# Moving GpSimd's element-wise work to VectorE in a two-layer hybrid decoder trunk

## The chip, the cores and the metric

The kernel runs on one core of a Trainium2 chip. The metric is the device time of one execution in microseconds; the median of several runs counts. The engines are called as the profile calls them: PE is TensorE (PEld its weight loads), DVE is VectorE, ACT is ScalarE, POOL is GpSimd, SP is SyncE, which issues the DMAs.

## The reference, cut to what matters

Two layers over 256 tokens of width 1024, all in float32. Each layer has four parts, each behind an RMSNorm and added to the residual stream:

```python
for i in range(DEPTH):
    h = h + 0.5 * swiglu(rms_norm(h, ffn1_norm[i]), ffn1_w_gate_up[i], ffn1_w_down[i])
    h = h + parallel_mixing(rms_norm(h, mix_norm[i]), mix_w_in[i], ...)
    h = h + memory_cross_attention(rms_norm(h, xa_norm[i]), rms_norm(mem, xa_mem_norm[i]), ...)
    h = h + 0.5 * swiglu(rms_norm(h, ffn2_norm[i]), ffn2_w_gate_up[i], ffn2_w_down[i])
return rms_norm(h, final_norm)
```

The mixing part is the one that matters here. It projects to three head groups, whose results are joined and projected back:

- A, a gated delta net with 4 heads of 128 in chunks of 64: a short causal convolution and silu on q, k and v, l2 normalization of q and k, beta = sigmoid, g = -exp(a_log) * softplus(a + dt_bias), per chunk the inverse of a unit lower triangular 64x64 matrix (`triangular_solve`), a state carried from chunk to chunk, then an RMSNorm with `dn_out_norm` (one gain for each of the 128 columns of a head) and a product with silu(z);
- B, softmax attention in three dilated windows, 4 heads of 64;
- C, spatial gating: gelu, a layer norm with gain and bias, a lower triangular 128x128 matrix for each of 4 groups, a product.

## The kernel before, in words

Activations lie transposed, features on the 128 partitions and the 256 tokens along the free dimension. All large products take weights that come from HBM in chunks of 128x2048 in two tiles `wr`. Each tile is split into a high part `wh` (ACT casts it to the faster matmul type fp32r) and a low part `wl` (raw minus high, one DVE tensor_tensor of 1024 columns); three matmuls, high by high, high by low and low by high, then give float32 accuracy. `wsplit`, `wchunk` and `pair` (line 770) do this; `pair` takes one chunk and makes two 128x256 results with 48 matmuls. Small products of the delta net run as plain float32 matmuls on PE (kind "f", or "fs" with 64 columns), those of weights as kind "r".

The program isn't emitted in the order in which it is written. Every operation is recorded by `Plan.add` (line 162) with an estimated time on its engine (`dur`) and until its result can be read (`lat`, for DVE 0.08 us longer than `dur`). `Plan.schedule` (line 190) is a list planner: it simulates the five engines, at every step takes the engine that can start first and among its ready operations the one with the highest rank (the length of the chain behind it). Its result is the fixed instruction order of each engine; the chip then keeps each engine's order and waits on semaphores. The planner holds off an operation with two SBUF operands on DVE while one runs on POOL and the other way round (`lock`, kind "2"), charges PE for going from kind "r" to "f" and back (`switch`, line 266), and can lower the rank of an operation that would make PE change its kind by `HOLD` (line 147, used in line 303; 0.0 here). Every instruction is emitted at line 369, so rows of the trace are told apart by tiles, not by lines.

POOL has these jobs on data, all in the mixing part (`mixing`, line 843): the low part of the second tile of six chunks in each layer (`pair(x, (None, GP))`, lines 854 and 920), the low parts of the memory keys (line 827), the products of the decay matrix E with the key norms (line 983), the masks `mb` for the five later rounds of the triangular inverse (line 1024), the scaling of the softmax (line 1151), the masked spatial weights (line 1187), gain and bias of the layer norm (lines 1201 and 1202) and the out gain on z (line 1227). It also sets small tiles to constants and computes x to the power -1/2 for the norms (`rsqrt`, line 632), on at most 8 columns.

The triangular inverse runs in rounds over blocks of 2 to 32 (LEVELS). A round has for each of two token tiles: four small products of `mb` with `tt` on PE (the trace's ps<-tc,Mb), two ACT copies into the halves of `q` (Q<-ps), four small products (ps<-Q,uc), two DVE subtractions on the two halves of the partitions (tc<-tc,ps) and four DVE transposes on the four blocks of 32 partitions (uc<-tc). The other weight chunks of the mixing part are there to fill PE meanwhile. `proj_add` ends the part and takes the delta net's four results last.

Of the kernel before, what the change touches and what calls it, by code (L numbers as in the profile page):

```python
# [10 lines left out]
F32 = mybir.dt.float32  # L11
F32R = mybir.dt.float32r
# [34 lines left out]
S_DT, S_AL = 88, 92  # L47
S_BA = 96
NS = S_BA

L_ZG, L_LG, L_LB, L_BS, L_WS = 0, 128, 384, 640, 896
NL = L_WS + 512
# [83 lines left out]
class Plan:  # L136
# [9 lines left out]
    KEEP = ("pg", "ps", "wh", "wl", "t")  # L146
    HOLD = 0.0

# [13 lines left out]
    def add(self, eng, method, args, kw, outs, ins, dur, lat, table=None, kind=None):  # L162
        i = len(self.ops)
        op = dict(i=i, eng=eng, method=method, args=args, kw=kw, dur=dur, lat=lat, table=table, kind=kind,
                  prio=self.boost, tiles=[], preds={}, succs=[])
        for views, wr in ((ins, False), (outs, True)):
# [23 lines left out]
    def schedule(self, fixed=None):  # L190
# [37 lines left out]
        dma_next, table, kind, feed = 0, None, None, 0.0  # L228
        lock = {"DVE": 0.0, "GP": 0.0}
        dmas = [o["i"] for o in ops if o["eng"] == "DMA"]  # L230
        for o in ops:
# [43 lines left out]
        while left:  # L275
            best = None
            for e, lst in ready.items():
# [7 lines left out]
                for o in lst:  # L285
                    st = slot_time(o)
                    if st is not None:
                        t = max(o["at"], st, free[e])
                        if o["kind"] == "2":
                            t = max(t, lock["GP" if e == "DVE" else "DVE"])  # L290
                        cands.append((t, o))
                if not cands:
# [31 lines left out]
            if o["kind"] == "2":  # L324
                lock[e] = t + dur
            ready[e].remove(o)
            if fixed:
# [16 lines left out]
            for j in o["succs"]:  # L344
                q = ops[j]
                q["at"] = max(q["at"], end + self.hop(o, q))
                q["n"] -= 1
                if not q["n"]:
                    ready[q["eng"]].append(q)
# [135 lines left out]
def trunk(tc, xT, memT, w, w2, ca_d, cb_d, sm_d, fin_d, lb_d, out):  # L485
    plan = Plan(tc)
    PE, ACT, DVE, GP, SY = Tensor(plan), Scalar(plan), Vector(plan, "DVE"), Vector(plan, "GP"), Queue(plan)
    with ExitStack() as ctx:
# [331 lines left out]
        def mem_keys(xm):  # L820
            rb = mem_r[1][0]
            KT = []
            for c in range(4):
                ps = pair(xm)
                k = S([2, T])
                DVE.tensor_tensor(k, ps, bc4(rb, 2), op=ALU.mult)
                KT.append(parts(k, GP))
            return KT
# [14 lines left out]
        def mixing(l, norm, nxt, xm):  # L843
# [9 lines left out]
            pgv = xstat256(x, [wsplit(raw) for raw in raws], 264)  # L853
            pk0 = pair(x, (None, GP))
            r, (rb, rb8) = norm.st.finish("h", (1.0, 0.125))
# [61 lines left out]
            def conv(n, ps0=None):  # L917
                res = []
                for c in range(2):
                    ps = ps0 if ps0 is not None and c == 0 else pair(x, (None, GP))  # L920
                    for e in range(2):
# [59 lines left out]
            for t in range(2):  # L981
                es = E[t]
                GP.tensor_tensor(es, es, bcl(rk[:, 4 * t:4 * t + 4]), op=ALU.mult)
                pb = hmm(lambda o, i: PE.matmul(
# [35 lines left out]
            for n, b in enumerate(LEVELS[1:]):  # L1020
                for t in range(2):
                    u, tt, q = Uc[t], Tc[t], Qc[t]
                    mb = plan.tile([P, NH, 64], F32, "Mb", 6)
                    GP.tensor_tensor(mb, Mc[t], bc4(cbs(C_LVL + 64 * (n + 1), 64)), op=ALU.mult)
                    ps = sbank([NH, 64])
# [108 lines left out]
            for t in (1, 0):  # L1134
                nk = P * (t + 1)
                for par in range(2):
# [13 lines left out]
                    DVE.reciprocal(den, den)  # L1150
                    GP.tensor_tensor(p, p, bcl(den, nk), op=ALU.mult)
                    for i in range(2):
# [19 lines left out]
            def gelu2(z):  # L1172
# [13 lines left out]
            wsm = S([NH, P])  # L1186
            GP.tensor_tensor(wsm, lb[:, L_WS:L_WS + 512].rearrange("p (a b) -> p a b", a=4),
                             bc4(cbs(C_TRIU)), op=ALU.mult)
            ps = sbank([2, T])
            for t in range(2):  # L1190
# [8 lines left out]
                DVE.tensor_scalar(rs, rs, 0.5, None, op0=ALU.mult)  # L1199
                DVE.tensor_scalar(gv_[:, t, :], gv_[:, t, :], mv[:, 0:1], rs, op0=ALU.subtract, op1=ALU.mult)  # L1200
                GP.tensor_tensor(gv_[:, t, :], gv_[:, t, :], lb[:, L_LG:L_LG + T], op=ALU.mult)
                GP.tensor_tensor(gv_[:, t, :], gv_[:, t, :], lb[:, L_LB:L_LB + T], op=ALU.add)
                for gi in range(NH):
# [16 lines left out]
            for t in range(2):  # L1220
                z = S([NH, P])
                zf = z.rearrange("p a b -> p (a b)")
                act(zf, pp[t], AF.Copy, scale=r[:, t:t + 1])
                th = S([NH, P])
                act(th, z, AF.Tanh, scale=0.5)
                DVE.scalar_tensor_tensor(z, th, 1.0, z, op0=ALU.add, op1=ALU.mult)
                GP.tensor_tensor(z, z, bc4(lb[:, L_ZG:L_ZG + P]), op=ALU.mult)
                zg.append(z)
# [4 lines left out]
            for c in range(2):  # L1233
                ps = sbank([2, T])
                for e in range(2):
                    for t in range(2):
                        PE.transpose(ps[:, e, tsl(t)], zg[t][:, 2 * c + e, :], ident)
                sh, sl = parts(ps)
                merged[2 * c:2 * c + 2] = [(sh[:, i, :], sl[:, i, :]) for i in range(2)]
# [78 lines left out]
def _pack(a):  # L1318
# [23 lines left out]
    for l in range(DEPTH):  # L1342
# [23 lines left out]
        for half in range(2):  # L1366
# [8 lines left out]
        al = np.broadcast_to(f["dn_a_log"][l], (P, 4))  # L1375
        small.append(np.concatenate(gc + [cw, dt, al], 1))
        bs = f["sg_b_spatial"][l]
        big.append(np.concatenate([
            np.broadcast_to(f["dn_out_norm"][l], (P, P)),
            np.broadcast_to(f["sg_norm_gain"][l], (P, T)),  # L1380
# [49 lines left out]
```

## Time and profile before

| | us |
|---|---|
| median of 3 runs | 1286.95 (1285.84 to 1287.96) |
| profiled execution | 1287.47 |
| its span | 1285.70 |
| PE busy | 1253.5 |
| DVE busy | 957.5 |
| ACT busy | 718.4 |
| POOL busy | 120.8 |

The granted TensorE clock is at its upper level through nearly all of the span. The span begins with the FFN of layer 0; the mixing part of layer 0 lies from about 200 to 375 us, that of layer 1 from about 830 to 1005 us, and POOL's work on data lies in these two. A row of a group gives engine, operation, output and inputs by tile names with their shapes, the count, the busy time and the mean time of one; a row of the timeline gives the start and the time taken by the instructions merged in it. A matmul is listed longer than it keeps PE, since the next one starts before it ends.

### The profile page before, as it was taken

How to read it: one execution, taken by the hardware profiler on the slowest of the kernel's cores; microseconds unless marked ns; L12 is line 12 of the kernel's file. 1: busy time of each engine (PE TensorE's matmuls, PEld its weight loads, DVE VectorE, ACT ScalarE, POOL GpSimd, SP SyncE). 2: the span in 40 equal slices, each digit the busy share in tenths (PEclk: the TensorE clock that was granted, in tenths of full speed). 3: DMA queues.
4: the chain of work that ended last, by engine and by line, in shares of the span. 5: the costliest groups of instructions: out<-in, count | busy, mean ns of one | idle time of the engine just before them, and what ended most of it. 6: DMA issues, size and time to landing. Idle time of an engine off the chain costs nothing.

```text
span 1285.7 us, 22163 instructions
## 1 busy us (share of the span) xinstructions
PE 1253.5 (97%) x8376; PEld 1129.8 (88%) x8376; DVE 957.5 (74%) x1711; ACT 718.4 (56%) x1286; POOL 120.8 (9%) x135
## 2 busy tenths in 40 slices
PE   7999999999999999999999999998999999999997
PEld 6888889988998988888988888998899989888886
DVE  6777867987775777777677776699867766777764
ACT  6565745735654565555456565466366455555552
POOL 1000002441300000000000000036022000000000
PEclk9999999999999999999999999999999999999998
DMA  6555764423345455556555566643243544555551
GB/s 223 192 189 199 243 204 162 151 99 115 116 165 164 130 177 186 192 172 202 189 180 189 189 200 201 212 163 103 98 132 118 182 161 130 182 182 195 182 193 68
DMA packets 60874, 216.27 MB, mean 168 GB/s; under 512 B 7136, under 2 KB 7520, under 8 KB 60640
## 3 DMA queue, kind: packets, MB, share of 16 engines
q1 hardware_dynamic: 60768, 214.86, 50.5%
q8 instruction: 66, 1.08, 0.4%
q14 instruction: 40, 0.33, 0.1%
HBM read 213.78 MB, written 1.05 MB: 167 GB/s over the span
## 4 chain that ended last, share of the span: by engine, by line
PE 57%; issue 16%; DVE 7%; ACT 1%; DMA 0%; POOL 0%; POOLq 0%; DVEq 0%; SPq 0%; ACTq 0%
PE pg L369 51%; PE ps L369 6%; DVE wl L369 2%; DVE S L369 1%; DVE uc L369 1%; DVE q L369 1%; DVE tc L369 1%; ACT wh L369 1%; DMA S<-memT 0%; POOL wl L369 0%; DVE xs L369 0%; DVE po L369 0%; DVE zz L369 0%; DVE xmx L369 0%; ACT S L369 0%
## 5 line engine op out<-in xcount | busy, mean ns | idle before, releaser
L369 DVE TENSOR_TENSOR wl<-wr,wh 128x1024 fp32r<-128x1024 f32 (+1 forms) x386 | 479.0, 1242 | 231.1 <-ACT wh L369 230.2
L369 ACT CAST wh<-wr 128x1024 fp32r<-128x1024 f32 (+2 forms) x398 | 415.0, 1044 | 418.2 <-issue 254.4
L369 PE MATMUL pg<-X,wh 128*128 128x512 f32 (+1 forms) x2240 | 635.9, 354 | 6.7 <-DVE t L369 6.5
L369 PE MATMUL pg<-X,wl 128*128 128x256 f32 x1824 | 485.1, 282 | 6.0 <-POOL xs L369 2.6
L369 PEld LDWEIGHTS pg<-X,wh 128*128 128x128 f32 x2240 | 382.2, 189 | 53.6 <-ACT wh L369 6.5
L369 PE MATMUL pg<-S,wh 128*128 128x256 f32 (+1 forms) x1560 | 386.7, 327 | 0.0
L369 PEld LDWEIGHTS pg<-X,wl 128*128 128x128 f32 x1824 | 344.5, 189 | 24.4 <-DVE wl L369 4.1
L369 PE MATMUL pg<-S,wl 128*128 128x256 f32 x1088 | 301.9, 282 | 0.5 <-DVE wl L369 0.5
L369 PEld LDWEIGHTS pg<-S,wh 128*128 128x128 f32 x1560 | 260.2, 189 | 24.9
L369 PEld LDWEIGHTS pg<-S,wl 128*128 128x128 f32 x1088 | 205.0, 188 | 3.9 <-DVE wl L369 1.5
L369 DVE TENSOR_TENSOR t<-t,pg 128x256 f32<-128x256 f32 x204 | 84.1, 415 | 3.4 <-ACT t L369 3.4
L369 ACT COPY t<-pg 128x256 f32<-128x256 f32 x204 | 73.9, 366 | 15.1 <-PE pg L369 15.1
L369 DVE TENSOR_TENSOR t<-t,t 128x256 f32<-128x256 f32 x157 | 66.0, 422 | 10.9 <-ACT t L369 3.0
L369 POOL TENSOR_TENSOR rch<-rv,one 128x2 f32<-128x2 f32 x9 | 7.4, 821 | 631.5 <-DVE rv L369 631.5
L369 DVE TENSOR_TENSOR t<-t,rbh 128x256 f32<-128x256 f32 x116 | 48.4, 420 | 0.9
L369 PE MATMUL pg<-wh,X 128*128 128x264 f32 (+2 forms) x192 | 47.4, 332 | 0.0
L369 PE MATMUL ps<-S,S 128*128 128x256 f32 (+4 forms) x384 | 47.0, 289 | 0.0
L369 PEld LDWEIGHTS ps<-S,S 128*128 128x128 f32 (+2 forms) x384 | 41.4, 178 | 2.6 <-issue 1.0
L369 ACT CAST S<-t 128x256 fp32r<-128x256 f32 x88 | 35.8, 408 | 10.1 <-DVE t L369 10.1
L369 ACT ACTIVATE t<-t 128x256 f32<-128x256 f32 x88 | 36.5, 420 | 7.8 <-DVE t L369 7.7
L369 PE MATMUL pg<-wh,S 128*128 128x512 f32 x128 | 40.6, 393 | 0.0
L369 DVE TENSOR_TENSOR S<-t,S 128x256 fp32r<-128x256 f32 x88 | 36.8, 419 | 1.9 <-ACT S L369 1.9
(175 smaller groups left out, 966.6 us busy)
## 6 DMA issues: line engine op xcount, KB each, us to landing
wr<-w SPq DMA_DIRECT2D x390, 512.0 KB, 3.3
wr<-w SPq DMA_DIRECT2D x4, 528.0 KB, 4.6
S<-memT SPq DMA_DIRECT2D x8, 256.0 KB, 6.4
lb<-lb SPq DMA_DIRECT2D x2, 704.0 KB, 6.5
one<-cb SPq DMA_DIRECT2D x1, 1248.0 KB, 6.1
one<-xT SPq DMA_DIRECT2D x4, 256.0 KB, 5.3
wr<-w SPq DMA_DIRECT2D x4, 256.0 KB, 5.5
out<-S SPq DMA_DIRECT2D x3, 256.0 KB, 2.4
```

The source lines that it names most:

```text
L369: getattr(self.engines[o["eng"]], o["method"])(*[real(a) for a in o["args"]], **{k: real(a) for k, a in o["kw"].items()})
```

## The change

All listed jobs of POOL go to DVE, except the out gain on z: that comes in as a per-partition scalar (`S_ON`) when the transposed z is copied out of PSUM, ACT taking the high part with a scale and DVE the low part with a scalar_tensor_tensor. The layer norm's gain and bias are worked into two scalar_tensor_tensor, in place of one tensor_scalar on DVE and two operations on POOL. POOL keeps the memsets and the powers. In the planner, DVE and ACT no longer start an operation on other partition rows than the one before until that one has ended (`rows`, `over`); HOLD goes from 0 to 2 us; and a PE result counts as ready for the next PE instruction as soon as PE is free.

```diff
-    HOLD = 0.0
+    HOLD = 2.0
@@ add
-                  prio=self.boost, tiles=[], preds={}, succs=[])
+                  prio=self.boost, tiles=[], preds={}, succs=[], rows=outs[0].box()[0:2] if isinstance(outs[0], View) else None)
@@ schedule
         lock = {"DVE": 0.0, "GP": 0.0}
+        rows, over = {"DVE": None, "ACT": None}, {"DVE": 0.0, "ACT": 0.0}
...
+                        if e in rows and rows[e] != o["rows"]:
+                            t = max(t, over[e])
...
+            if e in rows:
+                rows[e], over[e] = o["rows"], t + lat + 0.02
...
-                q["at"] = max(q["at"], end + self.hop(o, q))
+                q["at"] = max(q["at"], t + dur if e == q["eng"] == "PE" else end + self.hop(o, q))
@@ mem_keys
-                KT.append(parts(k, GP))
+                KT.append(parts(k))
@@ mixing
-            pk0 = pair(x, (None, GP))
+            pk0 = pair(x)
...
-                    ps = ps0 if ps0 is not None and c == 0 else pair(x, (None, GP))
+                    ps = ps0 if ps0 is not None and c == 0 else pair(x)
...
-                GP.tensor_tensor(es, es, bcl(rk[:, 4 * t:4 * t + 4]), op=ALU.mult)
+                DVE.tensor_tensor(es, es, bcl(rk[:, 4 * t:4 * t + 4]), op=ALU.mult)
...
-                    GP.tensor_tensor(mb, Mc[t], bc4(cbs(C_LVL + 64 * (n + 1), 64)), op=ALU.mult)
+                    DVE.tensor_tensor(mb, Mc[t], bc4(cbs(C_LVL + 64 * (n + 1), 64)), op=ALU.mult)
...
-                    GP.tensor_tensor(p, p, bcl(den, nk), op=ALU.mult)
+                    for i in range(2):
+                        DVE.tensor_scalar(p[:, i, :], p[:, i, :], den[:, i:i + 1], None, op0=ALU.mult)
...
-            GP.tensor_tensor(wsm, lb[:, L_WS:L_WS + 512].rearrange("p (a b) -> p a b", a=4),
+            DVE.tensor_tensor(wsm, lb[:, L_WS:L_WS + 512].rearrange("p (a b) -> p a b", a=4),
                              bc4(cbs(C_TRIU)), op=ALU.mult)
...
-                DVE.tensor_scalar(gv_[:, t, :], gv_[:, t, :], mv[:, 0:1], rs, op0=ALU.subtract, op1=ALU.mult)
-                GP.tensor_tensor(gv_[:, t, :], gv_[:, t, :], lb[:, L_LG:L_LG + T], op=ALU.mult)
-                GP.tensor_tensor(gv_[:, t, :], gv_[:, t, :], lb[:, L_LB:L_LB + T], op=ALU.add)
+                DVE.scalar_tensor_tensor(gv_[:, t, :], gv_[:, t, :], mv[:, 0:1], lb[:, L_LG:L_LG + T],
+                                         op0=ALU.subtract, op1=ALU.mult)
+                DVE.scalar_tensor_tensor(gv_[:, t, :], gv_[:, t, :], rs, lb[:, L_LB:L_LB + T],
+                                         op0=ALU.mult, op1=ALU.add)
...
-                GP.tensor_tensor(z, z, bc4(lb[:, L_ZG:L_ZG + P]), op=ALU.mult)
...
-                sh, sl = parts(ps)
+
+                g = smc[:, S_ON:S_ON + 1]
+                sh, sl = S([2, T], F32R), S([2, T], F32R)
+                act(sh, ps, AF.Copy, scale=g)
+                DVE.scalar_tensor_tensor(sl, ps, g, sh.bitcast(F32), op0=ALU.mult, op1=ALU.subtract)
```

The packing on the host moves `dn_out_norm` from the table `lb` (128 columns less) to the table `sm` (one column more).

## Rows read from the trace of the kernel before

**Rows 1.** The page: busy time of each engine, share of the span, instructions.

```profile
PE 1253.5 (97%) x8376; PEld 1129.8 (88%) x8376; DVE 957.5 (74%) x1711; ACT 718.4 (56%) x1286; POOL 120.8 (9%) x135
```

**Rows 2.** Stretches: length, then PE, PEld, DVE, ACT, POOL busy (count), clock, DMA.

```profile
220.00:240.00 20.00, 18.14 (x152) 17.79 (x151) 19.96 (x40) 12.69 (x24) 7.94 (x9) 1.00 0.47 154
240.00:260.00 20.00, 19.77 (x171) 19.58 (x171) 19.58 (x48) 14.66 (x32) 13.16 (x16) 1.00 0.42 136
260.00:280.00 20.00, 18.11 (x174) 16.72 (x173) 19.14 (x49) 6.56 (x16) 10.47 (x12) 1.00 0.24 83
...
300.00:320.00 20.00, 20.00 (x151) 17.88 (x150) 12.38 (x15) 11.82 (x19) 3.36 (x6) 1.00 0.36 110
...
500.00:520.00 20.00, 20.00 (x117) 17.50 (x116) 15.15 (x26) 11.83 (x22) 0.00 (x0) 1.00 0.57 185
```

**Rows 3.** Waits of PE's weight loads, 200 to 300: us, times, longest.

```profile
PEld ps L369 <- issue: 2.9, 6, 0.9
PEld pg L369 <- POOL xs L369: 2.4, 2, 2.1
PEld ps L369 <- ACT Q L369: 2.1, 4, 0.9
```

**Rows 4.** The same waits in layer 1, 840 to 940.

```profile
PEld ps L369 <- issue: 5.8, 8, 2.4
PEld pg L369 <- POOL wl L369: 1.6, 1, 1.6
PEld ps L369 <- ACT Q L369: 0.7, 2, 0.5
PEld pg L369 <- POOL xs L369: 0.6, 1, 0.6
```

**Rows 5.** Timeline (start, us taken): POOL and DVE at 212, DVE at 977.

```profile
212.33 2.40 POOL L369 TENSOR_TENSOR wl<-wr,wh 128x1024 fp32r<-128x1024 f32 x1 [3.74 <-ACT wh L369]
212.40 2.37 DVE L369 TENSOR_SCALAR zz<-ex 128x8 f32<-128x8 f32 x1
...
977.34 0.92 DVE L369 SCALAR_TENSOR_TENSOR S<-S,S 128x512 f32<-128x512 f32 x1
```

**Rows 6.** DVE groups by form: count, busy us, mean ns (wl: 480 to 640).

```profile
L369 DVE TENSOR_TENSOR wl<-wr,wh 128x1024 fp32r<-128x1024 f32 x57 | 69.8, 1225 | 40.8 <-ACT wh L369 40.8
...
L369 DVE TENSOR_TENSOR t<-t,t 128x256 f32<-128x256 f32 x157 | 66.0, 422 | 10.9 <-ACT t L369 3.0 <-DVE t L369 0.5
L369 DVE SCALAR_TENSOR_TENSOR X<-one,one,X 128x256 fp32r<-128x256 f32 x64 | 30.4, 479 | 0.0
L369 DVE STREAM_TRANSPOSE uc<-tc 32x128 f32<-32x128 f32 x64 | 19.4, 303 | 1.3
L369 DVE TENSOR_TENSOR S<-S,S 128x512 fp32r<-128x512 f32 x10 | 6.9, 687 | 1.4 <-ACT S L369 1.4
L369 DVE TENSOR_SCALAR S<-S,xden 128x256 f32<-128x256 f32 x16 | 5.1, 351 | 0.3
```

**Rows 7.** POOL groups by form, whole span.

```profile
L369 POOL TENSOR_TENSOR wl<-wr,wh 128x1024 fp32r<-128x1024 f32 x12 | 31.0, 2586 | 12.6 <-ACT wh L369 11.6 <-POOL xs L369 0.6
```

**Rows 8.** Timeline of layer 1 around 871: POOL, and PE behind it.

```profile
870.06 3.00 POOL L369 TENSOR_TENSOR wl<-wr,wh 128x1024 fp32r<-128x1024 f32 x1
...
873.11 0.39 PE L369 MATMUL pg<-X,wl 128*128 128x256 f32 x1 [1.37 <-POOL wl L369]
```

**Rows 9.** Timeline of DVE: two and eight instructions in a row.

```profile
227.40 0.87 DVE L369 SCALAR_TENSOR_TENSOR q<-xs,one,q 128x256 f32<-128x256 f32 x2
...
272.83 2.55 DVE L369 STREAM_TRANSPOSE uc<-tc 32x128 f32<-32x128 f32 x8
```

**Rows 10.** Timeline of PE: weight matmuls, then a run on 64 columns.

```profile
281.64 0.28 PE L369 MATMUL pg<-wl,X 128*128 128x256 f32 x1
281.76 0.28 PE L369 MATMUL pg<-wh,X 128*128 128x256 f32 x1
281.97 0.68 PE L369 MATMUL ps<-tc,Mb 128*64 128x64 f32 x8
```

More of the change, by code (lines that the diff above doesn't have):

```diff
@@ L47 @@
 S_DT, S_AL = 88, 92
-S_BA = 96
-NS = S_BA
-L_ZG, L_LG, L_LB, L_BS, L_WS = 0, 128, 384, 640, 896
+S_ON = 96
+NS = 97
+L_LG, L_LB, L_BS, L_WS = 0, 256, 512, 768
 NL = L_WS + 512
@@ L1375, in _pack @@
         al = np.broadcast_to(f["dn_a_log"][l], (P, 4))
-        small.append(np.concatenate(gc + [cw, dt, al], 1))
+        small.append(np.concatenate(gc + [cw, dt, al, f["dn_out_norm"][l][:, None]], 1))
         bs = f["sg_b_spatial"][l]
         big.append(np.concatenate([
-            np.broadcast_to(f["dn_out_norm"][l], (P, P)),
             np.broadcast_to(f["sg_norm_gain"][l], (P, T)),
```

## The prediction

> **What bounds the kernel now.** I read first the page's busy line: PE is busy 97% of the span, DVE 74%, ACT 56%, POOL 9% [rows 1]. So a change to POOL and DVE can only pay where PE waits for them. Next the table by stretches [rows 2]: in the FFN (500 to 520) PE is busy 20.00 of 20 us and POOL does nothing; there is nothing to gain there. In the mixing stage of layer 0, from 220 to 280, DVE is busy 58.7 of 60 us and PE is short of full. Here DVE is as much the bound as PE, and layer 1, 630 us later, repeats it. Then the waits of PE's weight loads, which stand for PE's own queue: 7.4 us between 200 and 300 [rows 3], 8.7 us between 840 and 940 [rows 4]. Together 16.1 us in 24 waits, and that is about all that this change can win: 1.25% of the span. Of it 4.6 us name POOL (2.4, 1.6 and 0.6); the other 11.5 us ("issue", ACT Q) lie around the small matmuls of the inverse (ps with tc, Mb, Q, uc).
>
> **What POOL does to DVE.** A 128x8 tensor_scalar, the smallest kind of DVE work there is, started 0.07 us after a POOL weight subtraction and took 2.37 us, as long as the POOL instruction's 2.40 [rows 5]. I compared each DVE instruction with the usual time of its form away from POOL: 35 of them are stretched, the first that zz, the last an S<-S,S of 0.92 us (0.69 is usual) [rows 5], by 30.9 us in all: 12.5 us at 200 to 300, 13.8 at 830 to 930, 4.3 after these stretches, 0.2 before. So part of DVE's 98% is waiting for POOL, counted as busy.
>
> **Part by part: DVE.** Gone: these 30.9 us, since POOL keeps only memsets and the few pow operations of 1 to 8 columns. Added, both layers together, priced at the undisturbed DVE rows [rows 6]: 12 weight subtractions (now 2.59 us each on POOL [rows 7]) at 1.225 = 14.7; 20 masks Mb at the 128x256 form's 0.422 = 8.4; 8 low parts of the memory keys at 0.687 = 5.5; 4 decay products and 2 masked spatial weights of 512 columns at 0.687 = 4.1; layer norm: 8 scalar_tensor_tensor at 0.479 in place of 4 tensor_scalar at 0.351 = +2.4; softmax scaling: 16 tensor_scalar at 0.351 = 5.6 (an upper price, since half have 128 columns). The out gain goes into the copies of the transposed z: a pointer scalar costs 0.06 us on DVE (0.479 against 0.422), for 4 DVE and as a guess also 4 ACT instructions, 0.5 us at most; its 4 POOL products vanish. Sum on DVE: +41 us, less 31, so +10 us net. Where does this lie? In 200 to 300 and 830 to 930 each layer gets 6 subtractions, 10 masks, 2 decay products and the layer norm: 7.4 + 4.2 + 1.4 + 1.2 = 14.2 us against 12.5 and 13.8 removed: +1.7 and +0.4 us. The remaining +8 us fall outside, mostly after 300, where DVE is busy 12.4 of 20 us (300 to 320) [rows 2]: I cost that at nothing, covered by DVE's idle time; without that cover it costs the 8 us. What comes in the saturated stretches I charge at half, +1 us: bounds 0 (its place in the queue is off the path) and +2.1.
>
> **The waits on POOL.** At 871.5 PE stopped 1.37 us for a POOL subtraction that took 3.00 us [rows 8]; on DVE it takes 1.225. All 4.6 us that name POOL go. What is late next is the DVE queue itself: work that had an engine of its own now stands behind an instruction of up to 1.2 us in a queue that is nearly always full. I give back 1 us of the 4.6: -3.6. Bounds: -4.6, and 0 if each of these subtractions queues as long as POOL took.
>
> **The ordering table.** The program's order is written out by a list planner that thinks a DVE instruction frees its engine 0.08 us before it ends. The trace shows this for instructions on the same 128 partitions: two scalar_tensor_tensor of 256 columns, 0.48 us each [rows 6], take 0.87 together [rows 9]. But eight transposes of 0.303 us, each on another block of 32 partitions [rows 6], take 2.55 us, 0.32 apart [rows 9]; the planner has them 0.21 apart. A layer has 40 such transposes and 16 half-height subtractions in the inverse, so the planner runs some 56 x 0.1 = 5.6 us ahead of the chip in each. PE is in order: a small matmul placed too early holds up the weight matmuls behind it, which are ready. That is what I read in the 11.5 us of other waits. The new rule makes the planner wait as the chip does, and the port stall that it only half knows goes with POOL. No row of before shows the new order. Bounds: 0 (the waits only move) and -11.5 (all filled). I take the middle, -5.8: filling needs split weights, which need the same DVE, and DVE stays full.
>
> **HOLD = 2.0** makes PE stay with a kind of matmul unless the other ranks 2 us higher. Going from a weight matmul to an fp32 one takes 0.21 us where matmuls follow each other 0.12 apart [rows 10]: 0.09 us extra. I count 11 short runs on 64 columns in each layer's inverse; halving them is worth about 11 x 0.09 = 1 us at best, -0.5 taken. The other bound is a rival below. The changed time at which a PE result is ready for PE itself alters nothing I can see: PE is free no earlier than that.
>
> **Sum.** -3.6 - 5.8 - 0.5 + 1 = -8.9 us. The profiled execution took 1287.47 us (span 1285.70), 0.5 above the median of the runs, 1286.95. 1287.47 - 8.9 = 1278.6; against the median it would be 1278.1. I say 1278.
>
> **Rivals.** (1) The stalls move and do not shrink. The inverse is a chain PE, ACT, PE, DVE; its transposes run back to back on DVE whatever the order, and PE may have nothing else ready. Then only the POOL waits go, and DVE's extra work and a new place to wait take them back: between 1285 and 1290. For it: DVE is 98% busy exactly there. Against: 4.4 us of the early chain (zz and one po, 2.2 us each above their usual time) in each layer vanish with POOL [rows 5], so DVE reaches the inverse sooner. Chance 0.14. (2) Slower: DVE becomes the bound. If the order can't use the regained 31 us where they arise (a stall removed off the path returns nothing) while the added instructions stand on the path, PE pays the net +10 us: 1297.5. It decides from the point at which DVE has no gap left past 280, and PE's waits then name DVE wl. Chance 0.12. The Trainium skill (Perfetto Trace Analysis, section Optimizing Scalar/DVE Operations) speaks for this rival: where DVE is saturated, moving some work to Scalar or even GPSIMD may make sense, and this change does the reverse. It adds that shifting work between DVE and GPSIMD might not help, as they share a read port; the stretched zz agrees with that half, and by the first half alone the sum would be that of this rival. (3) Slower: HOLD keeps the small matmuls back. The inverse has 5 rounds of two products; if each waits half of a 48-matmul weight pair (48 x 0.12 = 5.8 us, half 2.9), the chain ends 29 us later in each layer. About 10 such pairs, 58 us, are there as cover, so mostly it costs nothing; if a sixth isn't covered, 5 us a layer, 1297. Chance 0.06. The change does less than it says in one point: POOL keeps pow and memsets, so a few short stalls can remain; that is inside the 1 us given back.
>
> **How the numbers follow.** Forecast 0.68: PE waits less, 1267 to 1284 (all bounds together: -4.6 - 11.5 - 1 = -17 to 1270, and some 3 us more that the gaps hide, since a matmul is listed longer than its spacing; the other end -3.6 and nothing else). Rival 1: 0.14. Rivals 2 and 3: 0.18, at 1290 to 1300. The range 1266 to 1291 leaves out most of the last two and little below. 0.2%, or 2.6 us, is about what a measurement can tell: faster means under 1284.4, slower over 1289.5. Faster 0.68, same 0.14, slower 0.18.
>
> **What would show it.** Right: POOL's subtractions (31 us [rows 7]) and its other products gone; DVE's total near 967 us (957.5 now), zz well under 1 us and no wl above 1.3; PE's weight-load waits in the two mixing stretches falling from 16 to 6 or 7 us; the FFN stretches unchanged. Wrong: DVE full past 280 with PE waiting for wl (rival 2); waits of ps matmuls as long as before at other places (rival 1); fewer, longer runs of small matmuls and PE idle ahead of the projection at about 350 (rival 3); or a different time in the FFN, which I hold to be untouched.

## The result: 1269.85 us, and the profile after

| | before | after |
|---|---|---|
| median, us (4 runs each, on one chip) | 1287.34 (1285.84 to 1287.96) | 1269.85 (1269.56 to 1270.08) |
| ratio to before, 95% interval | | 0.9866 [0.9849, 0.9883] |
| span of the profiled execution, us | 1285.70 | 1267.8 |

The change makes the kernel 17.5 us faster, twice the 8.9 us of the forecast and inside its range. Throughout, `before` and `after` are the two kernels, and e1 to e13 the kernels of the experiments.

The page of after, busy time of each engine (against [rows 1]):

```profile
PE 1247.3 (98%) x8376; PEld 1126.3 (89%) x8376; DVE 954.1 (75%) x1777; ACT 722.7 (57%) x1290; POOL 26.7 (2%) x69
```

DVE has 66 more instructions and is busy 3.4 us less. POOL's 120.8 us have shrunk to 26.7, all of it constants (memsets) and powers.

The stretches of after, with the columns of [rows 2] (length, then PE, PEld, DVE, ACT, POOL busy with counts, clock, DMA):

```profile
220.00:240.00 20.00, 20.00 (x172) 20.00 (x171) 19.88 (x44) 16.50 (x32) 2.74 (x9) 1.00 0.55 181
240.00:260.00 20.00, 20.00 (x175) 20.00 (x174) 17.84 (x45) 15.33 (x25) 2.04 (x5) 1.00 0.47 151
260.00:280.00 20.00, 20.00 (x193) 19.26 (x192) 18.30 (x51) 7.91 (x18) 1.64 (x1) 1.00 0.26 87
...
300.00:320.00 20.00, 20.00 (x187) 19.00 (x184) 13.05 (x24) 10.20 (x22) 1.59 (x8) 1.00 0.34 110
...
500.00:520.00 20.00, 20.00 (x116) 17.49 (x115) 15.18 (x27) 11.61 (x22) 0.00 (x0) 1.00 0.53 185
```

From 220 to 280 PE is now busy all 60 us (56.0 in [rows 2]) and issues 540 matmuls where it issued 497. DVE, which was busy 58.7 of these 60 us, has some room: 56.0. The stretch at 500, in the FFN, is as before.

Waits of PE's weight loads in after, 200 to 300 (us, times, longest; against [rows 3]):

```profile
PEld ps L374 <- issue: 1.1, 3, 0.4
PEld ps L374 <- ACT Q L374: 0.4, 1, 0.4
PEld ps L374 <- PE pg L374: 0.4, 1, 0.4
```

That is 1.9 us where [rows 3] have 7.4. Layer 1, some 10 us earlier than before, has 2.1 us from 830 to 930 where [rows 4] have 8.7. No row of the two stretches names POOL.

The timeline of DVE in after (start, us taken): the small zz of [rows 5], and two groups of the triangular inverse (the eight transposes answer to [rows 9]):

```profile
210.00 0.17 DVE L374 TENSOR_SCALAR zz<-ex 128x8 f32<-128x8 f32 x1
...
280.11 1.08 DVE L374 TENSOR_TENSOR tc<-tc,ps 64x128 f32<-64x128 f32 x4
281.12 2.04 DVE L374 STREAM_TRANSPOSE uc<-tc 32x128 f32<-32x128 f32 x8
```

zz takes 0.17 us instead of 2.37. Of the 35 stretched DVE instructions with their 30.9 us, none is left. And, not foreseen, eight transposes take 2.04 us instead of 2.55.

To see where the time went I took the distance of each matmul's start from the next one's and summed what exceeds the median of its form. This excess is 65.5 us in before and 46.6 in after: 18.9 us less, near the change of the span (17.9). Of it 16.8 us lie in the two mixing parts (7.4 in layer 0, 9.3 in layer 1), taken from the first ps<-one,rch ahead of each part to the first behind it; the parts became 5.7 and 7.4 us shorter by these landmarks, with some ten matmuls more in each.

A part of this is the TensorE clock. In before PE stood still for 2.22 us in layer 1, and shortly after, from 901.5 to 905.0, the granted clock was at the lower of its two levels (0.91 is the mean of the 20 us in the row):

```profile
900.95 1.69 PE L369 MATMUL ps<-Q,uc 128*64 128x64 f32 x16 [2.22 <-DVE S L369]
...
890.00:910.00 20.00, 17.52 (x158) 16.19 (x157) 18.46 (x43) 6.14 (x16) 12.23 (x13) 0.91 0.30 101
```

The matmuls that start in these 3.5 us take 1.8 us longer than the medians of their forms, 1.8 of the 17.9 us as an estimate. In after the clock is at its upper level until the last 8 us of the span, which before has at the lower level too.

### The profile page after: what moved, and what is told of

Read it like the earlier page. It is cut to its first block, busy times and chain, and to the rows that moved or that the text cites. A ratio compares the mean times of both kernels' runs of the same rounds, so it can differ in the third digit from the quotient of the medians.

```text
span 1267.8 us, 22167 instructions
## 1 busy us (share of the span) xinstructions
PE 1247.3 (98%) x8376; PEld 1126.3 (89%) x8376; DVE 954.1 (75%) x1777; ACT 722.7 (57%) x1290; POOL 26.7 (2%) x69
## 4 chain that ended last, share of the span: by engine, by line
PE 76%; issue 15%; DVE 4%; ACT 2%; DMA 2%; SPq 1%; POOLq 0%; POOL 0%; DVEq 0%; ACTq 0%
PE pg L374 69%; PE ps L374 7%; DVE S L374 2%; DVE wl L374 2%; ACT S L374 1%; ACT wh L374 1%; DMA wr<-w 1%; SPq L374 1%; DMA one<-xT 1%; DMA S<-memT 0%; DVE t L374 0%; ACT L374 0%; ACT t L374 0%; DVE xmx L374 0%; DVE mx L374 0%
## 5 line engine op out<-in xcount | busy, mean ns | idle before, releaser
L374 DVE TENSOR_TENSOR wl<-wr,wh 128x1024 fp32r<-128x1024 f32 (+2 forms) x398 | 485.0, 1219 | 228.4 <-ACT wh L374 226.8
L374 ACT ACTIVATE t<-one 128x256 f32<-128x256 f32 x72 | 29.4, 413 | 12.2 <-DVE one L374 7.7
```

Of the source, the lines that this page charges most:

```text
L374: getattr(self.engines[o["eng"]], o["method"])(*[real(a) for a in o["args"]], **{k: real(a) for k, a in o["kw"].items()})
```

## The experiments

No kernel here leaves out any of the computation. The runs were taken in batches, each beside the kernel before, which had a median between 1286.7 and 1288.4 us; a difference of two times from different batches is uncertain by up to 1.7 us, and where it matters the ratio to before is used as well. The theory to be tested: the gain is two things, POOL's reads that no longer hold DVE up, and an order that knows that DVE waits between instructions on different rows. The rivals: the gain is the order alone (HOLD among it); the gain is the wait for POOL's results alone; or what costs is POOL's work as such and not its reads.

**The move alone (e1).** The operations of after with the planner of before:

```diff
-    HOLD = 2.0
+    HOLD = 0.0
...
-                        if e in rows and rows[e] != o["rows"]:
-                            t = max(t, over[e])
...
-                q["at"] = max(q["at"], t + dur if e == q["eng"] == "PE" else end + self.hop(o, q))
+                q["at"] = max(q["at"], end + self.hop(o, q))
```

> The operations of the changed kernel, planned with the old ordering table: HOLD 0, no rule for other partition rows, the old ready time on PE. Theory A (the prediction's: POOL waits and a planner that runs ahead in the inverse are two separate losses): only the POOL term and the extra DVE work act, -3.6 + 1, so about 1284.5, and PE's weight-load waits around the inverse stay near the 11.5 us of before. Theory B (POOL's stalls of DVE were the cause of both kinds of waits): nearly all of the gain is here, 1270 to 1273. Theory C (the ordering table alone makes the gain): 1287 or slower by DVE's net +10 us.

Measured: 1278.96 us, 0.9933 [0.9916, 0.995] of before. So the move by itself is worth 8.8 us: more than theory A expected (to about 1284.5), less than theory B (1270 to 1273). The lower clock of before in layer 1 is gone here too. The waits of PE's weight loads in this kernel, 200 to 300:

```profile
PEld ps L372 <- issue: 2.9, 6, 0.7
PEld ps L372 <- ACT Q L372: 1.1, 3, 0.5
PEld ps L372 <- PE ps L372: 0.6, 2, 0.4
```

The 2.9 us of "issue" are those of [rows 3], unchanged; POOL's 2.4 us are gone and ACT Q has lost 1.0. So waits around the small matmuls are what the move leaves for the order.

**The planner alone (e2).** The operations of before with the class `Plan` of after.

> The operations of the kernel before, POOL's work kept, planned with the new ordering table and HOLD 2. Theory A: the order term -5.8 and HOLD -0.5, so about 1281; the waits that name POOL (4.6 us) and the 30.9 us by which DVE is stretched stay. Theory B: within 3 us of 1287, since stalls that the planner can't foresee keep PE waiting whatever the order. Theory C: 1270 to 1273.

Measured: 1287.52 us, 1.0001 [0.9992, 1.001]. Nothing: theory A's 1281 failed. DVE's transposes are paired here too in part (28 overlaps of the kind counted under e4, where after has 54). The waits of PE's weight loads, 200 to 300:

```profile
PEld ps L374 <- issue: 2.8, 5, 1.5
PEld pg L374 <- POOL xs L374: 2.0, 1, 2.0
PEld ps L374 <- POOL S L374: 1.7, 1, 1.7
PEld ps L374 <- DVE S L374: 0.5, 1, 0.5
```

DVE is still stretched, by 36.9 us in 39 instructions, and PE waits for POOL by name. The better order needs POOL out of the way. Together with e1 this is a table of four: 1287.3 with neither, 1279.0 with the move, 1287.5 with the planner, 1269.85 with both. The planner is worth nothing while POOL works on data and 9.1 us when it doesn't. Why it is quite nothing in the first case is argued from these rows and not shown.

**HOLD (e3) and the row rule (e4), each taken out of after.**

```diff
-    HOLD = 2.0
+    HOLD = 0.0
```

> The changed kernel with HOLD back at 0, rule for rows kept. Theory A: HOLD is worth 0.5 us, so 1270.4; at most 1 us. Rival: HOLD is a large part of what the prediction missed, because PE changes its kind of matmul fewer times and DVE is left to get ahead: 1274 to 1279, with the short runs of small matmuls near 11 a layer again.

Measured: 1272.43 us, 0.988 [0.9865, 0.9895]. HOLD is worth some 2.6 us (1.8 by the ratios), more than theory A's 1 us at most and less than the rival's; the intervals of the two ratios overlap.

```diff
-                        if e in rows and rows[e] != o["rows"]:
-                            t = max(t, over[e])
```

> The changed kernel without the rule for other partition rows, HOLD 2 kept. Theory A: loses the order term, -5.8 expected and, by the measured result, up to 11.5: 1275 to 1281, with PE waiting around the inverse (ps products of tc, Mb, Q, uc) as before. Theory B: 1270 to 1272, since without POOL's stalls the planner's error of 0.1 us an instruction is small.

Measured: 1277.84 us, 0.9923 [0.9908, 0.9938]: the rule is worth 8.0 us, most of the 9.1, as theory A has it. In the profiled execution the clock fell once, from 933.4 to 936.9 us, which made its matmuls 1.6 us longer. What the rule does is seen in one group of DVE by form (count, busy us, mean ns), first without the rule, then in after:

```profile
L372 DVE STREAM_TRANSPOSE uc<-tc 32x128 f32<-32x128 f32 x64 | 19.4, 303 | 1.3
```

```profile
L374 DVE STREAM_TRANSPOSE uc<-tc 32x128 f32<-32x128 f32 x64 | 15.9, 281 | 0.6
```

Without the rule the 64 transposes keep DVE for 64 times their own length; with it, for 3.5 us less. The rule makes the planner put the same block of the two token tiles one behind the other, and these overlap: of the 112 row-bound instructions of the inverse 54 start before the one ahead has ended, against none in before, 4 in e1 and 2 without the rule. Their mean distance is 0.26 us, against 0.31 without the rule and 0.33 in before. In all, DVE is busy 954.1 us with the rule and 960.0 without it. How much of the 8.0 us comes from these pairs and how much from a planner whose times are nearer to the chip's, no run separates.

**Work on POOL that nobody waits for (e7).** Everything as in after, the order on PE, DVE and ACT too, but with twelve subtractions of 1024 columns on POOL whose result is not used (`cb` holds constants; the 0.05 us keep the planner from seeing them). Neither waits for the other by a semaphore, so a rival by which only the waits for POOL's results cost time expects nothing from this.

```diff
+            if ghost:
+                hi = res[1][0][:, 0:4].bitcast(F32)
+                mark = tiny("mark", [4])
+                plan.add("GP", "tensor_tensor", (mark, hi, hi), dict(op=ALU.subtract), [mark], [hi], 0.05, 0.05)
+                o = plan.tile([P, 1024], F32, "gh", 1)
+                a, b = cb[:, 0:1024], cb[:, 1024:2048]
+                plan.add("GP", "tensor_tensor", (o, a, b), dict(op=ALU.subtract), [o], [a, b], 0.05, 0.05)
```

> The changed kernel with PE, DVE and ACT in exactly the same order, and 12 more POOL instructions: a subtraction of 1024 columns of constants into a tile that nobody reads, started where POOL's 12 weight subtractions were started before. It adds no work to any other engine and nobody waits for its result. Theory D (after the first four runs: what the move brings is that POOL no longer holds DVE up, and the ordering rule can only act once DVE's times can be foreseen): DVE instructions are stretched by 10 to 20 us in all, as before, and the time rises by 5 to 12 us, to 1275 to 1282. Rival E (the move's gain is the shorter latency of the moved results, 1.2 for 2.6 us, not the stalls): within 2 us of 1270, since no result comes later.

Measured: 1295.07 us, 1.0058 [1.0041, 1.0074], 25.2 us above after. They did not run where that text puts them: they needed only the constants and ran one after another from 127 to 159 us, in the FFN. The timeline there, POOL and DVE, then PE:

```profile
127.02 32.07 POOL L374 TENSOR_TENSOR gh<-one 128x1024 f32<-128x1024 f32 x12 [112.97 <-DMA one<-cb]
130.47 0.41 DVE L374 TENSOR_TENSOR t<-t,pg 128x256 f32<-128x256 f32 x1
133.04 2.65 DVE L374 TENSOR_TENSOR S<-t,S 128x256 fp32r<-128x256 f32 x1
135.61 2.63 DVE L374 TENSOR_TENSOR t<-t,t 128x256 f32<-128x256 f32 x1
138.17 2.57 DVE L374 TENSOR_TENSOR t<-t,rbh 128x256 f32<-128x256 f32 x1
...
149.19 0.58 PE L374 MATMUL pg<-X,wl 128*128 128x256 f32 x1 [15.53 <-DVE wl L374]
...
160.56 0.58 PE L374 MATMUL pg<-S,wl 128*128 128x256 f32 x1 [6.89 <-DVE wl L374]
```

Instructions of 0.42 us take as long as POOL's, 2.65: each waits for one whole subtraction and gets in between two of them. The one with an operand in PSUM (t<-t,pg) takes its usual 0.41. In all 12 DVE instructions are longer by 25.4 us: even in the FFN, where DVE has idle time, PE runs out of split weights in a burst of this length. It stops twice, for 22.4 us, and both waits are put down to "DVE wl". That the kernel pays 25.2 us, nearly DVE's 25.4, is a coincidence, since a part of it is the clock, which fell to its lower level while PE stood still (stretch of e7, columns of [rows 2]; in after it has 57 matmuls and a clock of 1.00):

```profile
140.00:150.00 10.00, 0.81 (x3) 0.72 (x4) 10.00 (x5) 2.99 (x5) 9.69 (x5) 0.50 0.00 0
```

It was at that level from 138.7 to 152.3 and from 155.7 to 166.0 us, and the matmuls that ran in these stretches took 4.1 us longer than the medians of their forms. Rival E is out. Theory D's range is missed, and e12 repeats the run in the place that was meant.

**The weight subtractions back on POOL (e8), or only they moved (e9).** The first, e8, is after with

```diff
-            pk0 = pair(x)
+            pk0 = pair(x, (None, GP))
...
-                    ps = ps0 if ps0 is not None and c == 0 else pair(x)
+                    ps = ps0 if ps0 is not None and c == 0 else pair(x, (None, GP))
```

> The changed kernel, planned anew, with only the 12 weight subtractions back on POOL; masks, decay products, layer norm, softmax and the rest stay on DVE, which loses 14.7 us of work. Theory D: these 12 made 20 of the 30.9 us of stretched DVE time, so much of the move's gain goes: 1277 to 1284. Rival F (the masks and decay products on POOL, which hold DVE up inside the inverse, are the larger part): 1270 to 1274.

Measured: 1274.68 us, 0.9893 [0.9878, 0.9908], 4.8 us above after. Ten DVE instructions are stretched, by 20.0 us, while DVE is spared 12 x 1.224 = 14.7 us of subtractions: 5.3 us more of DVE's time, for 4.8 us (3.5 by the ratios, and the intervals overlap). The stretch is not the only cause here: waits of PE's weight loads that name POOL (xs and wl, 3.8 us in the two mixing stretches) are back as well. The time lies between theory D (1277 to 1284) and rival F (1270 to 1274), nearer to F.

The second, e9, takes the other half: before's operations and after's planner, and of the moves only the reverse of the diff above.

> The kernel before with the new ordering table and only the 12 weight subtractions moved to DVE; everything else stays on POOL (60 us of it). Theory D: the larger part of the move's gain, 1274 to 1280, with the masks still stretching DVE in the inverse. Rival F: 1282 to 1288.

Measured: 1281.13 us, 0.9946 [0.9931, 0.9961], 11.3 us above after, and between the ranges of theory D and rival F. The small jobs left on POOL stretch 27 DVE instructions by 16.8 us. With the new planner the four kernels run at 1287.5 (all on POOL), 1281.1 (weights moved), 1274.7 (the others moved) and 1269.85: the weight subtractions bring 4.8 to 6.4 us, the other jobs 11.3 to 12.8, depending on which goes first (3.5 to 7.1 and 10.3 to 13.9 by the ratios). The small jobs weigh more for each microsecond of stretch, probably because they also stand in the chain of the inverse (POOL Mb, in layer 1, and POOL S are among e2's waits).

**The unused subtractions in their place (e12).** As in e7, but each held to its chunk: the small subtraction writes into the tile of the large one.

```diff
-                mark = tiny("mark", [4])
+                mark = o[:, 0:4]
```

> As the run before with 12 unused POOL subtractions of constants, and PE, DVE and ACT again in exactly the order of the changed kernel, but each one now starts when its weight chunk has been cast in the mixing part, six in each layer (in the run before they all ran between 127 and 157 us, where they found the constants loaded, held DVE up by 25.4 us and cost 25 us). POOL's own memsets and powers queue behind them. Theory D: DVE stretched by 15 to 25 us, in stretches where it has little to spare; the time rises by 8 to 20 us, to 1278 to 1290. Rival E: within 2 us of 1270.

Measured: 1286.09 us, 0.9994 [0.9984, 1.0004]: all of the gain is gone, 16.2 us above after, with the order of PE, DVE and ACT unchanged and nothing waiting for POOL. The timeline in the mixing part of layer 0, and the waits of PE's weight loads from 830 to 930:

```profile
217.66 0.47 DVE L374 SCALAR_TENSOR_TENSOR q<-xs,one,q 128x256 f32<-128x256 f32 x1
217.80 2.60 POOL L374 TENSOR_TENSOR gh<-one 128x1024 f32<-128x1024 f32 x1
218.06 2.36 DVE L374 SCALAR_TENSOR_TENSOR po<-po,z 128x8 f32<-128x8 f32 x1
```

```profile
PEld pg L374 <- DVE wl L374: 5.1, 5, 2.0
PEld ps L374 <- DVE ngc L374: 2.8, 1, 2.8
PEld ps L374 <- issue: 0.7, 2, 0.4
```

A product of 8 columns takes 2.36 us (0.16 is usual). Twelve DVE instructions are longer, by 20.1 us. PE's waits name DVE's results (wl for 10.0 us in the two mixing stretches) and never POOL. Here too the clock has a share: it fell for 3.4 us in each layer (from 237.4 and from 882.6 us), behind stops of PE of 1.74 and 2.64 us, and the matmuls in these stretches took 3.0 us longer than the medians of their forms. The order is one that was planned without this work, so 16.2 us is its price in an order that does not know of it.

**The old ready time for PE (e10).**

```diff
-                q["at"] = max(q["at"], t + dur if e == q["eng"] == "PE" else end + self.hop(o, q))
+                q["at"] = max(q["at"], end + self.hop(o, q))
```

> The changed kernel with the old time at which a PE result counts as ready for the next PE instruction. The prediction says that it alters nothing on the chip: 1269 to 1271. Rival: it shifts ties and with them the order, by 2 us or more either way.

Measured: 1272.47 us, 0.989 [0.9875, 0.9905], 2.6 us above after, with overlapping intervals; if the difference is real, it is the rival's. Counted by tiles (pg, then ps), PE goes from weight matmuls to small ones 84 times (66 in after), and 24 times for a single one (4 in after): the line does change the order.

**A milder row rule (e11) and a larger HOLD (e6).** The row rule with the start block of 32 partitions only, in place of the exact rows:

```diff
-rows=outs[0].box()[0:2]
+rows=outs[0].box()[0] // 32
```

> The changed kernel with a milder rule in the planner: DVE and ACT wait only where the output begins in another block of 32 partitions than the one before, not where the number of rows alone differs. If the chip holds an instruction only for another start block, this plan is nearer to it: 1266 to 1270. If it also holds those of another height, 1270 to 1273.

Measured: 1270.54 us, 0.9872 [0.9858, 0.9887]. No difference from after, so whether the chip looks at the start or at all of the rows stays open. And HOLD doubled:

```diff
-    HOLD = 2.0
+    HOLD = 4.0
```

> The changed kernel with HOLD 4. Going from 0 to 2 brought 2.6 us. If each change of matmul kind costs and the inverse has cover to spare, 4 brings up to 1 us more: 1268.5 to 1270. If rival 3 of the prediction holds beyond 2 us (small matmuls kept back, chain late), slower: 1272 to 1276.

Measured: 1268.89 us, 0.9866 [0.9851, 0.9881]. No difference either.

**Reads or mere work? (e13)** Each unused subtraction of e12 becomes three memsets of the same tile, which write but read nothing:

```diff
-                plan.add("GP", "tensor_tensor", (o, a, b), dict(op=ALU.subtract), [o], [a, b], 0.05, 0.05)
+                for _ in range(3):
+                    plan.add("GP", "memset", (o, 0.0), {}, [o], [], 0.02, 0.02)
```

> As the run with 12 unused POOL subtractions in place, PE, DVE and ACT in the same order as ever, but each subtraction replaced by three memsets of 1024 columns, which read nothing (about 0.9 us each by the memset rows of 128 and 256 columns, so POOL is busy as long). POOL's own memsets and powers queue behind them as before. Theory D (POOL's reads hold DVE up): hardly any DVE instruction is stretched, 1269 to 1273. Rival G (the 16 us came from the small POOL jobs that queued behind the added ones): 1282 to 1288, with DVE instructions at their usual times.

Measured: 1268.75 us, 0.986 [0.9842, 0.9877]: as after. POOL's group, then the timeline at the first of them:

```profile
L374 POOL MEMSET gh<- 128x1024 f32 x36 | 34.6, 962 | 2.0
```

```profile
211.62 0.16 DVE L374 TENSOR_SCALAR po<-z 128x8 f32<-128x8 f32 x1
211.81 2.98 POOL L374 MEMSET gh<- 128x1024 f32 x3
212.29 0.16 DVE L374 SCALAR_TENSOR_TENSOR po<-po,z 128x8 f32<-128x8 f32 x1
213.44 1.21 DVE L374 TENSOR_TENSOR wl<-wr,wh 128x1024 fp32r<-128x1024 f32 x1
```

34.6 us of POOL, more than the subtractions' 31.8, and the two-input instructions beside it (po, wl) take their usual 0.16 and 1.21. Of the tensor_tensor and scalar_tensor_tensor without an operand in PSUM, 42 start during a memset here and none is longer; in e12, 11 of the 14 that start during a subtraction are, and none of the ten with an operand in PSUM. A tensor_scalar of 512 columns at 833.72 is held by a memset (1.23 us instead of 0.42). So it is POOL's reads that hold up these two-input instructions, and with e12 this is shown: 16.2 us for reads, nothing for writes, in the same order of PE, DVE and ACT. Rival G is out.

No variant is faster than after by more than its interval.

## Why the prediction was right or wrong

**The bound: right.** PE's waits in the mixing stage fell and the FFN stayed. But 16.1 us "and that is about all that this change can win" was too low a roof: the listed waits fell by 12.1 us, to 4.0, and the span by 17.9. The list holds what PE's queue waits for by name; the excess between matmuls (65.5 us before, 46.6 after) is the fuller account, and the time at the lower clock, some 1.8 us in layer 1 of before, is in the second and not in the first. Nor do the names hold: the longest wait of "issue" in [rows 4], 2.4 us, is one for DVE S in PE's own row (900.95). The stop of 1.37 us began at 871.7, not 871.5, which changes nothing.

**What POOL does to DVE: right in kind, mis-sized in time.** That POOL's work made DVE instructions longer was read from [rows 5], and e12 and e13 show it as the cause. The forecast then priced it by the waits that name POOL, 4.6 us, and gave 1 us back: -3.6, with +1 for DVE's added work. Measured for the move alone: -8.8, of which some 1.8 can be the clock. This is the first step that failed: a held DVE instruction makes PE wait for DVE, so the name POOL stands on a part of the cost only. In e12 no wait of PE's weight loads carries it, and the kernel is 16.2 us slower. The 12.5 and 13.8 us of stretch that the prediction counted in the two saturated stretches were nearer the scale of the gain than the waits, though not a price either: e7 and e12 paid for stretch and for the clock.

**DVE's added work: the prices held.** The groups of after that answer to them:

```profile
L374 DVE TENSOR_TENSOR wl<-wr,wh 128x1024 fp32r<-128x1024 f32 x390 | 477.2, 1224 | 226.0 <-ACT wh L374 224.4
L374 DVE TENSOR_TENSOR Mb<-mc,one 128x256 f32<-128x256 f32 x20 | 7.4, 418 | 0.1
L374 DVE TENSOR_SCALAR S<-S,den 128x256 f32<-128x256 f32 x8 | 2.4, 344 | 0.0
L374 DVE TENSOR_SCALAR S<-S,den 128x128 f32<-128x128 f32 x8 | 1.9, 284 | 0.1
```

wl at 1.224 us (1.225 taken), masks at 0.418 (0.422), the softmax scaling at 4.3 in all (5.6 as an upper price). Counted as single durations, all of DVE's instructions sum up to 6.9 us more than before; forecast was 10. Yet the busy time fell from 957.5 to 954.1, against 967 forecast: the other 10 us are instructions that now overlap. The prediction had no overlap gained in this sum. Of it 5.9 us are the row rule's (960.0 busy without it), the next point; the rest is there with the move alone (960.2 busy in e1, with 1045.0 in single durations).

**The order: right in kind, too small, and in part for another reason.** This is the second step that failed. Taken was -5.8, with -0.5 for HOLD and 0 for the ready time; the planner measured -9.1 on top of the move, of which the row rule is 8.0, inside its bounds (0 to -11.5). The prediction saw the rule as a correction of the planner's estimates, 56 x 0.1 us in a layer, and wrote that the transposes "run back to back on DVE whatever the order". They don't: a planner that charges for other rows puts equal ones in pairs, and the chip then does overlap them. ScalarE gains in the same way: of its 44 copies into Q, 20 start in after before the one ahead has ended, 6 without the rule. Four of them in before, then in after:

```profile
268.60 1.11 ACT L369 COPY Q<-ps 64x128 f32<-64x128 f32 x4 [1.42 <-PE ps L369]
```

```profile
271.38 0.83 ACT L374 COPY Q<-ps 64x128 f32<-64x128 f32 x4
```

The Trainium skill (VectorE: DVE Perf Modes, section Two Vector instructions with no wait between them) states a rule that fits DVE's part: an instruction is held until every earlier one has finished when an input starts in another quadrant of 32 partitions than the last read of the same memory, or its output in another than the last write. The distances in the inverse, 0.31 to 0.33 us on changing blocks and 0.26 with the pairs, agree; e11 could not tell start quadrant from exact rows.

That the planner is worth nothing while POOL works (e2) was not foreseen: the two terms were added as if independent. In that sense -5.8 was the price of an edit that alone is worth 0.

**HOLD and the ready time.** HOLD: -0.5 taken, -2.6 measured. The bound of 1 us rested on 0.09 us for a change of kind and 11 runs a layer. By the distances of starts in after, a run on 64 columns between weight matmuls costs about 0.24 us beyond its matmuls. Changes of kind, counted as under e10, fell from 95 in before to 78 in e1 and 66 in after; without HOLD they are 76. Ten changes at 0.24 us are 2.4 us, an estimate near HOLD's 2.6. The ready time was held to alter nothing; it is probably worth 2.6 us through the order. With intervals that overlap neither of these two is certain.

**The sum.** The range held, in part by luck. The move (-8.8) lies beyond the bounds given to its terms, -4.6 at best; HOLD and the ready time, if real, lie beyond theirs; the order alone is worth 0. Only the row rule lies inside. The result is where the prediction put all bounds taken together (1270), and the range was wide enough for it. The clock stands in no term.

**The rivals.** Stalls only move (1285 to 1290): no, the waits shrank from 16.1 to 4.0 us. DVE becomes the bound (1297.5): no; from 220 to 280 DVE is still busy 56.0 of 60 us, but PE's weight loads wait 4.0 us in the two mixing stretches and never for wl there. The Trainium skill's advice that spoke for this rival (Perfetto Trace Analysis, section Optimizing Scalar/DVE Operations: with a saturated DVE, offloading some work, even to GpSimd, may make sense) does not hold here. Its second half does, that for the shared read port the offload might not help: e8, which offloads a third of the moved work again at 14.7 us off DVE, gets 20.0 us of stretch for it and is 4.8 us slower. HOLD keeps small matmuls back (1297): no, and not at 4.0 either.

The Trainium skill (SBUF — State Buffer, section Who interferes with whom) states the mechanism: only the shared pair of ports causes contention, it is an exclusive lock, and a DVE instruction with two SBUF inputs contends with a GpSimd one that reads SBUF, not with one that only writes. e12 and e13 agree with both halves, and so does t<-t,pg in e7, with one input in PSUM and its usual 0.41 us. The sentence on two inputs does not cover the tensor_scalar that were held: zz in before and po<-z in e12 by a read, S<-S in e13 by a write. Why they were held, no run here tests.

## What to carry to other kernels

A DVE instruction that is held up by a GpSimd read shows as a longer instruction, not as a wait: compare each with the usual time of its form, and look for the price of GpSimd's work in that stretch, in the stages where DVE is full, not in the waits that name GpSimd. Work on another engine is only worth having if it takes more off DVE than it adds in stretch; and a better order may be worth nothing until that is out of the way, so try two such edits together as well as singly. Read the granted clock of a stretch in which PE stopped before the loss is put down to the stop alone. A planner that writes the order should know which instructions overlap on the chip, since its order can then bring them together.

## What the runs showed of the hardware that was not expected

- GpSimd's twelve reads of 2.6 us each held up twelve DVE instructions by 25.4 us in the FFN, where the kernel then took 25.2 us longer, 4.1 us of it by the estimate at the lower clock; in the mixing part twelve instructions by 20.1 us cost 16.2, of which 3.0 at the lower clock. Even an instruction of 8 columns is held for nearly the whole of a read (2.36 us for 0.16).
- A stop of PE can cost more than its own length: after 2.22 us in before and after 1.74 and 2.64 us in e12 the granted clock was at its lower level for about 3.5 us, and the matmuls in it took 1.5 to 1.8 us longer. What decides it these runs do not show: after stops of 1.82 us in e2 and e8 and 1.86 in before the clock stayed up, and in e4 it fell at 933.4 us with no such stop just ahead.
- Memsets on GpSimd for 34.6 us cost no time. One DVE tensor_scalar of 512 columns beside them took 1.23 us instead of 0.42, the only such case seen.
- ScalarE overlaps its copies on equal rows as DVE does its instructions: four on halves of the partitions in 0.83 us instead of 1.11.
